# A hybrid decoder layer on one core: the mixers' TensorE order written out by hand

## The chip, the cores and the metric

The kernel runs on one core of a Trainium2 chip. The metric is the device time of one execution in microseconds. The kernel before took 2433.67 us (median of 3 runs, 2430.02 to 2435.79). One more execution was profiled. Engines are called PE (TensorE), DVE (VectorE), ACT (ScalarE), POOL (GpSimd) and SP (which issues the DMAs).

## What is computed

One decoder layer for 1024 prompt tokens and 8 x 8 sample tokens (1088 columns in all), model width 1024:

```
x = x + 1/2 * post1(SwiGLU_1(pre1(x)))
z = pre2(x) @ w_in                      # one input projection for everything below
branch A: sliding-window (128) attention, 8 heads on 2 key heads, with sinks
branch B: causal conv (width 4) and SiLU on q, k, v; gated DeltaNet, 4 heads of 128, chunks of 64
m = (sigmoid(gA) * (oA @ w_branch_a) + sigmoid(gB) * (oB @ w_branch_b)) @ w_out
x = x + post2(m)
x = x + 1/2 * post3(SwiGLU_2(pre3(x)))
```

Branch B solves, for each chunk and head, a unit lower triangular system, and then carries a 128 x 128 state S through the chunks:

```
sol = triangular_solve(I + M, [k * beta * exp(gc), v * beta])     # M strictly lower
v_new = v_u - k_cum @ S
o = q_dec @ S + (q k^T * decay) @ v_new
S = S * g_tot + k_dec^T @ v_new
```

## The kernel before, in words

All activations stand with features on partitions and the 1088 tokens along the free axis, in three chunks of 384, 384 and 320 columns (`CH`). Large products are made in three passes of split operands (high and low parts, lines 140 to 142 in `gemm`); the products of attention and of the delta heads are full-precision ones.

The kernel has five stages: the first FFN, keys, values and queries (lines 717 to 728), the mixers (834 to 1352), the branch and output projections (1358 to 1420), the second FFN. The change lies in the mixers.

The input projection's other columns are handled in *units* of 128 columns: a unit loads two weight tiles, splits each on ACT (line 113) and DVE (114) and makes 24 products for each of the three chunks. `conv_unit` (964) does one of 12 q, k or v columns with the convolution (line 980 for its taps, 1008 for the SiLU), `z_unit` (1015) one of 4 output gates, `gate_unit` (1042) one of 16 branch gates.

Attention over the prompt (`attention_prompt`, 907) has 16 items (8 blocks of 128 queries, two groups of four heads). `att_s` makes an item's scores, adds the mask on DVE (862) and runs the softmax (819): a maximum (822) on DVE, exponents on ACT (828), the division by the sum on ACT (832). `att_o` transposes the probabilities on PE (883), copies them (888) and multiplies with the values (893). The program issues the scores of an item, then the output of the item before. `attention_sample` (916) does the same for the sample tokens, four small items one after the other.

`delta_head` (1047) does one head: transposes and norms of k, the decay matrices D (1105, exponents 1113 and 1114), q k and k k products (1102, 1122), the matrix M (1126). The 32 x 32 diagonal blocks of M go to DRAM and come back one block to a partition, 34 of them (1161 to 1165); 31 steps of two DVE operations (1180, 1186) invert them all at once; the inverse and its transpose go out and come back into the zeroed tiles L and U (1187 to 1198). Two rounds of products make 128 x 128 inverses of them (1211 to 1230), with U scaled chunk by chunk on DVE (1202) and ACT (1203). Then comes the scan over eight chunks:

```
1253-1255  p[:, 0:128]    = U v, then + M S
1257       vns (DVE)      = p[:, 0:128] * kds
1259       vn  (ACT)      = p[:, 0:128]
1260       p[:, 128:256]  = k vns
1263       S2  (DVE)      = S * gtot + p[:, 128:256]
1270-1271  po[:, 0:128]   = S q, then + vn QK      # a PSUM tile of its own
1272       QK  (ACT)      = po[:, 0:128]
```

The sample tokens follow (1276 to 1309) and the gated norm (1311 to 1323), which ends with a product on POOL and a store (`obd`).

What sets the order: a scheduler of the framework places every instruction of every engine by its priority (program order, with some raised) and by a model of when its inputs are ready. So PE's order in the mixers is a mix that it chooses: gemm products of later units stand among the full-precision products of attention and of the heads. The program's order is attention, then head by head conv units, delta head, and z and gate units between (1329 to 1352). Only in attention do extra dependencies fix the order of some products. PSUM: three tiles for gemms (`pa`), two each of `ph` and `py`, one `po`; heads 0 and 2 use `ph` alone, heads 1 and 3 `py` alone.

Of the kernel before, what the change touches and what calls it, by code (L numbers as in the profile page):

```python
# [35 lines left out]
def body(ctx: ExitStack, tc: tile.TileContext, d):  # L36
# [23 lines left out]
    bd = [dp.tile([34, 32, 32], F32, tag=f"bd{i}", name=f"bd{i}") for i in range(12)]  # L60
# [758 lines left out]
    def softmax(s3, sk, sm):  # L819
        j = s3.shape[1]  # L820
        m, neg, e, l, r = (sm[:, 4 * i : 4 * i + j] for i in range(5))
        nc.vector.tensor_reduce(out=m, in_=s3, op=ALU.max, axis=AX.X)
        nc.vector.tensor_tensor(out=m, in0=m, in1=sk, op=ALU.max)
        nc.vector.tensor_tensor(out=e, in0=sk, in1=m, op=ALU.subtract)
        nc.vector.tensor_scalar_mul(neg, m, -1.0)
        nc.scalar.activation(e, e, AF.Exp)
        for i in range(j):
            nc.scalar.activation(s3[:, i, :], s3[:, i, :], AF.Exp, bias=neg[:, i : i + 1], accum_out=l[:, i : i + 1])
# [5 lines left out]
    items = [(n, tp2) for n in range(8) for tp2 in range(2)]  # L834
    pos = {}
    masked = []
    SYNC = mybir.DependencyInfo(mybir.DependencyClass.Sync, mybir.DependencyReason.DATA)
    NOSYNC = mybir.DependencyInfo(mybir.DependencyClass.NoSync, mybir.DependencyReason.DATA)
    chain = []
    half2 = (slice(0, 64), slice(64, 128))  # L840

    def att_s(it):
        n, tp2 = items[it]
        k0 = 128 if n == 0 else 0
        ps = (ph(), py())
        for j in range(2):
            for g2, hs in enumerate(half2):
                mm = nc.tensor.matmul(
                    ps[g2][:, j * 256 + k0 : j * 256 + 256],
                    YA[tp2 * 2 + j][hs, n * P : n * P + P],  # L850
                    kT[hs, (n - 1) * P + k0 : (n + 1) * P],
                    start=True,
                    stop=True,
                )
                if masked:
                    tc.add_manual_dep(mm.ins, masked[-1], SYNC, reason="both halves start together")
                if chain:
                    tc.add_manual_dep(mm.ins, chain[-1], NOSYNC, reason="halves in turn")
                chain.append(mm.ins.name)
        s4 = sbs[it % 2][:, :1024].rearrange("p (h k) -> p h k", k=256)[:, :, k0:256]  # L860
        for g2 in range(2):
            mask = nc.vector.tensor_tensor(
                out=s4[:, 2 * g2 : 2 * g2 + 2, :],
                in0=ps[g2].rearrange("p (j k) -> p j k", k=256)[:, :, k0:256],
                in1=cst[:, C_AM + k0 : C_AM + 256].unsqueeze(1).to_broadcast([P, 2, 256 - k0]),
                op=ALU.add,
            )
        masked.append(mask.ins.name)
        softmax(s4, vec[:, V_SK + 4 * tp2 : V_SK + 4 * tp2 + 4], st())

    def att_o(it):
        n, tp2 = items[it]
        sb = sbs[it % 2]
        if n not in pos:
            pos[n] = po_tile()
        po = pos[n]
        h2s = (1,) if n == 0 else (0, 1)
        pt = (ph(), py())
        for g2 in range(2):
            for h2 in h2s:  # L880
                for j in range(2):
                    c0 = (2 * g2 + j) * 256 + h2 * P
                    mm = nc.tensor.transpose(pt[g2][:, h2 * 256 + j * P : h2 * 256 + j * P + P], sb[:, c0 : c0 + P], ident)
                    tc.add_manual_dep(mm.ins, chain[-1], NOSYNC, reason="behind the scores")
                    chain.append(mm.ins.name)
        ptb = pts[it % 2]
        copies = [
            nc.scalar.copy(ptb[:, g2 * 512 + h2s[0] * 256 : g2 * 512 + 512], pt[g2][:, h2s[0] * 256 : 512]) for g2 in range(2)
        ]
        for h2 in h2s:  # L890
            blk = n - 1 + h2
            for g2, hs in enumerate(half2):
                mm = nc.tensor.matmul(
                    po[hs, tp2 * 256 : tp2 * 256 + 256],
                    vtok[:, blk * P + hs.start : blk * P + hs.stop],
                    ptb[:, g2 * 512 + h2 * 256 : g2 * 512 + h2 * 256 + 256],
                    start=h2 == h2s[0],
                    stop=h2 == 1,
                )
                tc.add_manual_dep(mm.ins, copies[1].ins.name, SYNC, reason="both halves start together")  # L900
                tc.add_manual_dep(mm.ins, chain[-1], NOSYNC, reason="halves in turn")
                chain.append(mm.ins.name)
        if tp2 == 1:
            for t in range(4):
                nc.scalar.copy(YA[t][:, n * P : n * P + P], po[:, t * P : t * P + P])

    def attention_prompt():
        for it in range(len(items)):
            att_s(it)
            if it > 0:  # L910
                att_o(it - 1)
        att_o(len(items) - 1)
        for t in range(4):
            nc.sync.dma_start(oad[t, :, :NPR], YA[t][:, :NPR])

    def attention_sample():
        kc, vc = YA[5], YA[7]
        nc.sync.dma_start(vc[:, :NPR].rearrange("p (b c) -> p b c", c=P), d["vc"].rearrange("b k c -> k b c"))
        nc.sync.dma_start(kc[:, :NPR].rearrange("p (b c) -> p b c", c=P), d["kc"])
        pos = po_tile()  # L920
        for it in range(4):
            bg2, g2 = it // 2, it % 2
            lo, hi = 64 * g2, 64 * g2 + 64
            ps = py()
            for b4 in range(4):
                b = bg2 * 4 + b4
                ql = qs[lo:hi, b, :, :].rearrange("p t k -> p (t k)")
                nc.tensor.matmul(ps[32 * b4 : 32 * b4 + 32, 0:128], ql, kc[lo:hi, b * P : b * P + P], start=True, stop=True)
                nc.tensor.matmul(ps[32 * b4 : 32 * b4 + 32, 128:192], ql, kT[lo:hi, NPR:NT], start=True, stop=True)
            sb = YA[6][:, it * 256 : it * 256 + 192]  # L930
            nc.vector.tensor_tensor(out=sb[:, 0:128], in0=ps[:, 0:128], in1=cst[:, C_SMC : C_SMC + P], op=ALU.add)
            nc.vector.tensor_tensor(
                out=sb[:, 128:192], in0=ps[:, 128:192], in1=cst[:, C_SMN + bg2 * NSM : C_SMN + bg2 * NSM + NSM], op=ALU.add
            )
            softmax(sb.unsqueeze(1), vec[:, V_SKS + g2 : V_SKS + g2 + 1], st())
            pt = py()
            nc.tensor.transpose(pt[:, 0:128], sb[:, 0:128], ident)
            nc.tensor.transpose(pt[:NSM, 128:256], sb[:, 128:192], ident)
            ptb = YA[0][:, it * 256 : it * 256 + 256]
            nc.scalar.copy(ptb[:, 0:128], pt[:, 0:128])  # L940
            nc.scalar.copy(ptb[:NSM, 128:256], pt[:NSM, 128:256])
            nc.tensor.matmul(
                pos[lo:hi, bg2 * 128 : bg2 * 128 + 128], vts[:, lo:hi], ptb[:NSM, 128:256], start=True, stop=False
            )
            for b4 in range(4):
                b = bg2 * 4 + b4
                nc.tensor.matmul(
                    pos[lo:hi, bg2 * 128 + 32 * b4 : bg2 * 128 + 32 * b4 + 32],
                    vc[:, b * P + lo : b * P + hi],
                    ptb[:, 32 * b4 : 32 * b4 + 32],  # L950
                    start=False,
                    stop=b4 == 3,
                )
        obs = YA[1][:, :256]
        nc.vector.tensor_copy(
            obs.rearrange("p (t b k) -> p t b k", t=4, b=8), pos[:, :256].rearrange("p (b t k) -> p t b k", t=4, b=8)
        )
        nc.sync.dma_start(oad[:, :, NPR:NT].rearrange("t p q -> p t q"), obs.rearrange("p (t q) -> p t q", t=4))


    ncv = s2b.tile([P, 12, 3], F32, tag="ncv", name="ncv")
    nc.vector.memset(ncv, 0.0)

    def conv_unit(u, dst):
        w = unit(U_QKV + u, f"qkv{u}")
        cw = [vec[:, V_CW + u * 4 + j : V_CW + u * 4 + j + 1] for j in range(4)]
        for c, (a, b) in enumerate(CH):
# [4 lines left out]
            gemm(ps, w, xn2, c)  # L972
# [39 lines left out]
    eps4 = s2b.tile([P, 1], F32, tag="eps4", name="eps4")  # L1012
    nc.vector.memset(eps4, 4.0 * P * EPS * EPS)

# [324 lines left out]
    for i in range(0, 2):  # L1339
        gate_unit(i)  # L1340
# [210 lines left out]
```

## Time and profile before

| | us |
|---|---|
| median of 3 runs | 2433.67 |
| the profiled execution | 2440.89 |
| its span, first to last instruction | 2439.1 |
| mixers, first score product to last gate product | 851 to 1474 |

In the lines below, `L1186` is line 1186 of the kernel before. A row of the groups gives line, engine, operation, output and inputs by name, shapes, count, then busy time and mean ns of one, then the idle time of the engine before them and what ended it. A row of the stretches gives the stretch and its length, then PE, PE's weight loads, DVE, ACT and POOL (busy us and instructions), then the granted share of the PE clock, the DMA share and GB/s. A row of the timeline gives start, length, engine, line and operation. A full-precision 128 x 128 product leaves two records, so the timeline shows it as x2.

### The profile page before, as it was taken

How to read it: one execution, taken by the hardware profiler on the slowest of the kernel's cores; microseconds unless marked ns; L12 is line 12 of the kernel's file. 1: busy time of each engine (PE TensorE's matmuls, PEld its weight loads, DVE VectorE, ACT ScalarE, POOL GpSimd, SP SyncE). 2: the span in 40 equal slices, each digit the busy share in tenths (PEclk: the TensorE clock that was granted, in tenths of full speed). 3: DMA queues.
4: the chain of work that ended last, by engine and by line, in shares of the span. 5: the costliest groups of instructions: out<-in, count | busy, mean ns of one | idle time of the engine just before them, and what ended most of it. 6: DMA issues, size and time to landing. Idle time of an engine off the chain costs nothing.

```text
span 2439.1 us, 38987 instructions
## 1 busy us (share of the span) xinstructions
PE 2373.7 (97%) x14535; PEld 2291.1 (94%) x14535; DVE 1704.9 (70%) x3519; ACT 1127.3 (46%) x2344; POOL 50.9 (2%) x36
## 2 busy tenths in 40 slices
PE   8999999999999999989999999999999999999997
PEld 7999999999998988888898899999999999999997
DVE  8887657757788576679697226556997576676677
ACT  7644423323465478634544333246654333233344
POOL 0000000000000000011111000000000000000000
PEclk9999999999999999999999999999999999999998
DMA  8332212213453311322223345435532122122453
GB/s 270 121 117 87 69 51 86 70 51 96 166 187 125 123 40 46 105 75 85 94 79 102 94 157 167 130 117 204 164 98 93 57 74 78 52 78 81 154 166 132
DMA packets 161558, 264.67 MB, mean 109 GB/s; under 512 B 35028, under 2 KB 66232, under 8 KB 161360
## 3 DMA queue, kind: packets, MB, share of 16 engines
q1 hardware_dynamic: 161368, 262.18, 33.3%
q8 instruction: 114, 1.87, 0.3%
q14 instruction: 76, 0.62, 0.1%
HBM read 223.88 MB, written 39.21 MB: 108 GB/s over the span
## 4 chain that ended last, share of the span: by engine, by line
PE 48%; DVE 6%; DMA 1%; ACT 1%; issue 1%; SPq 0%; POOL 0%; DVEq 0%; ACTq 0%; POOLq 0%
PE pa L140 7%; PE pa L142 7%; PE pa L141 7%; PE pa L464 4%; PE pa L465 4%; PE pa L466 4%; PE ph L346 2%; PE ph L347 2%; PE py L347 2%; PE py L346 2%; PE py L345 2%; PE ph L345 2%; DVE s L1186 1%; DVE s L1180 1%; DVE t L980 1%
## 5 line engine op out<-in xcount | busy, mean ns | idle before, releaser
L464 PE MATMUL pa<-ch,h_c_s 128*128 128x384 f32 x704 | 237.4, 337 | 4.3 <-DVE t L470 3.9
L465 PE MATMUL pa<-cl,h_c_s 128*128 128x384 f32 x704 | 236.4, 336 | 4.7 <-DVE cl L274 4.7
L466 PE MATMUL pa<-ch,l_c_s 128*128 128x384 f32 x704 | 236.3, 336 | 0.0
L470 DVE TENSOR_TENSOR t<-pa,t 128x384 f32<-128x384 f32 x308 | 170.0, 553 | 84.4 <-PE pa L466 84.3
L464 PE MATMUL pa<-ch,h_c_a 128*128 128x384 f32 x528 | 177.1, 335 | 1.2 <-ACT t L382 0.8
L466 PE MATMUL pa<-ch,l_c_a 128*128 128x384 f32 x528 | 176.7, 335 | 0.0
L465 PE MATMUL pa<-cl,h_c_a 128*128 128x384 f32 x528 | 176.6, 335 | 0.0
L113 ACT CAST h_c_a<-r_c_a 128x512 fp32r<-128x512 f32 x132 | 81.8, 620 | 131.5 <-PE pa L465 113.3
L464 PEld LDWEIGHTS pa<-ch,h_c_s 128*128 128x128 f32 x704 | 132.9, 189 | 7.9 <-DVE t L470 7.4
L465 PEld LDWEIGHTS pa<-cl,h_c_s 128*128 128x128 f32 x704 | 133.0, 189 | 4.9 <-DVE cl L274 4.9
L466 PEld LDWEIGHTS pa<-ch,l_c_s 128*128 128x128 f32 x704 | 132.9, 189 | 0.0
L113 ACT CAST h_c_s<-q_c_s 128x512 fp32r<-128x512 f32 x132 | 82.0, 621 | 106.4 <-PE pa L465 95.8
L140 PE MATMUL pa<-xbh,h_ga 128*128 128x384 f32 (+1 forms) x384 | 129.3, 337 | 0.0
L142 PE MATMUL pa<-xbh,l_ga 128*128 128x384 f32 (+1 forms) x384 | 128.8, 335 | 0.0
L141 PE MATMUL pa<-xbl,h_ga 128*128 128x384 f32 (+1 forms) x384 | 128.3, 334 | 0.0
L464 PEld LDWEIGHTS pa<-ch,h_c_a 128*128 128x128 f32 x528 | 99.1, 188 | 2.1 <-ACT t L382 1.1
L466 PEld LDWEIGHTS pa<-ch,l_c_a 128*128 128x128 f32 x528 | 99.1, 188 | 0.0
L465 PEld LDWEIGHTS pa<-cl,h_c_a 128*128 128x128 f32 x528 | 99.1, 188 | 0.0
L140 PE MATMUL pa<-xbh,h_qkv 128*128 128x384 f32 (+1 forms) x288 | 96.7, 336 | 0.0
L141 PE MATMUL pa<-xbl,h_qkv 128*128 128x384 f32 (+1 forms) x288 | 96.4, 335 | 0.0
L142 PE MATMUL pa<-xbh,l_qkv 128*128 128x384 f32 (+1 forms) x288 | 96.2, 334 | 0.0
L113 ACT CAST h_c_s<-r_c_s 128x512 fp32r<-128x512 f32 x44 | 27.4, 623 | 147.7 <-PE pa L465 135.7
(615 smaller groups left out, 7340.9 us busy)
## 6 DMA issues: line engine op xcount, KB each, us to landing
r_c_a<-in_up_dram SPq DMA_DIRECT2D x132, 256.0 KB
q_c_a<-in_up_dram SPq DMA_DIRECT2D x44, 256.0 KB
q_ub<-in_up_dram SPq DMA_DIRECT2D x44, 256.0 KB
r_ub<-in_up_dram SPq DMA_DIRECT2D x44, 256.0 KB
r_ua<-in_up_dram SPq DMA_DIRECT2D x42, 256.0 KB
q_ua<-in_up_dram SPq DMA_DIRECT2D x42, 256.0 KB
r_da<-in_dn_dram SPq DMA_DIRECT2D x40, 256.0 KB
q_da<-in_dn_dram SPq DMA_DIRECT2D x40, 256.0 KB
```

The lines of the kernel that those rows point to most:

```text
L113: nc.scalar.copy(hi, full)
L140: nc.tensor.matmul(ps[:, :n], hi[:, j, :], at(xh, k), start=first, stop=False)
L141: nc.tensor.matmul(ps[:, :n], hi[:, j, :], at(xl, k), start=False, stop=False)
L142: mm = nc.tensor.matmul(ps[:, :n], lo[:, j, :], at(xh, k), start=False, stop=last)
L345: nc.tensor.matmul(ps[:, :n], hi[:, i, :], hh, start=i == 0, stop=False)
L346: nc.tensor.matmul(ps[:, :n], hi[:, i, :], hl, start=False, stop=False)
L347: nc.tensor.matmul(ps[:, :n], lo[:, i, :], hh, start=False, stop=i == len(hs) - 1)
L464: nc.tensor.matmul(ps, wh[:, k, :], xh[:, k, :], start=k == 0, stop=False)
L465: nc.tensor.matmul(ps, wh[:, k, :], xl[:, k, :], start=False, stop=False)
L466: nc.tensor.matmul(ps, wl[:, k, :], xh[:, k, :], start=False, stop=k == 3)
L470: nc.vector.tensor_tensor(out=out, in0=ps, in1=other, op=ALU.add)
L980: nc.vector.scalar_tensor_tensor(out=acc[:, :m], in0=pre[:, j : j + m], scalar=cw[j], in1=acc[:, :m], op0=ALU.mult, op1=ALU.add)
```

## The change

PE's order in the mixers is written by hand: the block runs under `manual_schedule` for PE, so that PE's instructions keep the program's order. The other engines and the DMAs are still ordered by the scheduler.

- Units become generators that yield after each k step of a chunk (three products) the time it is counted at. A queue of units is worked off by `fill(us)`, which takes steps from the first unit of the queue until that much time is counted, and by `finish`, which runs units to their end.
- Attention runs as a pipeline of three items: scores of item `it`, values of `it-2`, transposes of `it-1`, then a fill of 4.8. The division by the sum moves from ACT to one DVE product with a broadcast. The sample part makes all four scores and softmaxes, then all transposes, then all value products, with fills of 3.0, 8.0 and 2.0.
- The delta heads run in pairs (0 and 1, 2 and 3). Each head is two generators, `first` (to the matrix M and the transposed v) and `second` (the rest), and `together` advances both heads of a pair step by step. The number that a step yields is the fill behind it: 2.0 once in `first`, 2.0, 2.0 and 5.0 in `second`, 0.0 elsewhere, through the whole scan.
- One inversion serves a pair: 68 blocks on 68 partitions, with a fill of 46.0. The inverse goes to DRAM tiles that hold whole 128 x 128 matrices (zeroed once at the start, eight stores of 0.5 MB) and L and U are read back as whole rows. The inverse's tiles no longer overlap L and U; each head has a second half-tile (R2).
- In `second`, both halves of a head (four chunks each) go through each step before the next one. One DVE product with a broadcast replaces four scalings of line 1202. In the scan, the next chunk's U v product stands ahead of the k product, and the outputs go to columns 256 to 384 of the same PSUM tile.
- PSUM tiles of the heads alternate between `ph` and `py`.

Its core (unchanged or merely moved lines left out):

```diff
+    def gemm_p(ps, w, c):
+        for k in range(KT):
+            gemm(ps, w, xn2, c, ks=(k,), ends=(k == 0, k == KT - 1))
+            yield 0.0013 * width(c) + 0.04
+    def fill(us):
+        while us > 0 and queue:
+            t = next(queue[0], None)
+            if t is None:
+                queue.pop(0)
+            else:
+                us -= t
...
-        for i in range(j):
-            nc.scalar.mul(s3[:, i, :], s3[:, i, :], r[:, i : i + 1])
+        nc.vector.tensor_tensor(out=s3, in0=s3, in1=r.unsqueeze(2).to_broadcast(list(s3.shape)), op=ALU.mult)
...
+        for it in range(n + 2):
+            if it < n:
+                att_s(it)
+            if it >= 2:
+                att_v(it - 2)
+            if 1 <= it <= n:
+                att_t(it - 1)
+            fill(4.8 if it else 7.0)
...
+            def uv(c):
+                w, cs, ix = chunk_of(c, h)
+                ps[c] = pb()
+                nc.tensor.matmul(ps[c][:, 0:128], U[:, cs], v[:, cs], start=True, stop=c == 0)
+            uv(0)
+            yield 0.0
+            for c in range(8):
+                w, cs, ix = chunk_of(c, h)
+                p = ps[c]
+                if c > 0:
+                    nc.tensor.matmul(p[:, 0:128], M[:, cs], S, start=False, stop=True)
+                vns = ar[:, c % 2, :]
+                nc.vector.tensor_scalar_mul(vns, p[:, 0:128], tk["kds"][:, ix : ix + 1])
+                vn = ar[:, 2 + c % 2, :]
+                nc.scalar.copy(vn, p[:, 0:128])
+                yield 0.0
+                if c < 7:
+                    uv(c + 1)
+                yield 0.0
+                nc.tensor.matmul(p[:, 128:256], k[:, cs], vns, start=True, stop=True)
+                S2 = ar[:, 4 + c % 2, :]
...
+                if c > 0:
+                    nc.tensor.matmul(p[:, 256:384], S, q[:, cs], start=True, stop=False)
+                nc.tensor.matmul(p[:, 256:384], vn, QK[:, cs], start=c == 0, stop=True)
+                nc.scalar.copy(QK[:, cs], p[:, 256:384])
+                S = S2
+                yield 0.0
...
+    def together(a, b):
+        for us in zip(a, b):
+            fill(max(us))
...
+        for i, x in enumerate(heads):
+            h, L, U = x.h, x.A[1], x.A[5]
+            nc.sync.dma_start(blocks32(ud[h]), Md[34 * i : 34 * i + 32])
+            nc.sync.dma_start(bu[h][32:34], Md[34 * i + 32 : 34 * i + 34])
+            nc.sync.dma_start(blocks32(ld[h]), Ld[34 * i : 34 * i + 32])
+            nc.sync.dma_start(U[:, :NPR].rearrange("p (c s) -> p c s", s=P), whole_rows(ud[h]))
+            nc.sync.dma_start(L[:, :NPR].rearrange("p (c s) -> p c s", s=P), whole_rows(ld[h]))
...
+        fill(46.0)
...
+    with tc.manual_schedule(engines={mybir.EngineType.PE}):
+        queue += zs[0:2] + gates[0:3] + heads[0].conv
+        attention_prompt()
+        attention_sample()
+        queue += heads[1].conv
+        for hs in (heads[0:2], heads[2:4]):
+            finish(list(queue))
+            queue += gates[3:9] if hs[0].h == 0 else gates[9:]
+            together(*(x.first() for x in hs))
+            invert(hs)
+            together(*(x.second() for x in hs))
+            if hs[0].h == 0:
+                finish(list(queue))
+                queue += zs[2:4] + heads[2].conv + heads[3].conv
+        finish(list(queue))
+        wg4 = [unit(U_GA + i, f"ga{i}") for i in range(14, 16)]
+        for c in range(3):
+            for i in range(2):
+                drain(gate_do(14 + i, wg4[i], c))
```

More of the change, by code (lines that the diff above doesn't have):

```diff
@@ L59, in body @@
     zd = dp.tile([4, P, NT], F32, tag="zd", name="zd")
[L60 removed]
+    bm, bu = ([dp.tile([34, 32, 32], F32, tag=f"{n}{h}", name=f"{n}{h}") for h in range(4)] for n in ("bm", "bu"))
+    ld, ud = ([dp.tile([8, 4 * 4128], F32, tag=f"{n}{h}", name=f"{n}{h}") for h in range(4)] for n in ("ld", "ud"))
     yd = [dp.tile([P, 4, width(2)], F32, tag=f"yd{i}", name=f"yd{i}") for i in range(2)]
@@ L830, in softmax @@
         nc.vector.reciprocal(r, l)
-        for i in range(j):
-            nc.scalar.mul(s3[:, i, :], s3[:, i, :], r[:, i : i + 1])
[L834 to L958, printed above, removed]
@@ L964, in conv_unit, with finish @@
+    def finish(units):
+        for u in units:
+            if u in queue:
+                queue.remove(u)
+                drain(u)
     def conv_unit(u, dst):
@@ L971, in conv_unit @@
             ps = pa()
-            gemm(ps, w, xn2, c)
+            yield from gemm_p(ps, w, c)
             pre = t1()
@@ L1019, in z_unit @@
             ps = pa()
-            gemm(ps, w, xn2, c)
+            yield from gemm_p(ps, w, c)
             z = t1()
@@ L1031, in gate_do @@
         ps = pa()
-        gemm(ps, w, xn2, c)
+        yield from gemm_p(ps, w, c)
         z = t1()
@@ new lines, in gate_unit, with att_s @@
+            yield from gate_do(i, w, c)
+    items = [(n, tp2) for n in range(8) for tp2 in range(2)]
+    pos = {}
+    masked = []
+    probs = {}
+    half2 = (slice(0, 64), slice(64, 128))
+    def att_s(it):
+        n, tp2 = items[it]
+        k0 = 128 if n == 0 else 0
+        ps = (ph(), py())
+        for j in range(2):
+            for g2, hs in enumerate(half2):
+                mm = nc.tensor.matmul(
+                    ps[g2][:, j * 256 + k0 : j * 256 + 256],
+                    YA[tp2 * 2 + j][hs, n * P : n * P + P],
+                    kT[hs, (n - 1) * P + k0 : (n + 1) * P],
+                    start=True,
+                    stop=True,
+                )
+                if masked:
+                    tc.add_manual_dep(mm.ins, masked[-1], SYNC, reason="both halves start together")
+        s4 = sbs[it % 2][:, :1024].rearrange("p (h k) -> p h k", k=256)[:, :, k0:256]
+        for g2 in range(2):
+            mask = nc.vector.tensor_tensor(
+                out=s4[:, 2 * g2 : 2 * g2 + 2, :],
+                in0=ps[g2].rearrange("p (j k) -> p j k", k=256)[:, :, k0:256],
+                in1=cst[:, C_AM + k0 : C_AM + 256].unsqueeze(1).to_broadcast([P, 2, 256 - k0]),
+                op=ALU.add,
+            )
+        masked.append(mask.ins.name)
+        softmax(s4, vec[:, V_SK + 4 * tp2 : V_SK + 4 * tp2 + 4], st())
@@ new lines, in att_t @@
+    def att_t(it):
+        n, tp2 = items[it]
+        sb = sbs[it % 2]
+        h2s = (1,) if n == 0 else (0, 1)
+        pt = (ph(), py())
+        for g2 in range(2):
+            for h2 in h2s:
+                for j in range(2):
+                    c0 = (2 * g2 + j) * 256 + h2 * P
+                    nc.tensor.transpose(pt[g2][:, h2 * 256 + j * P : h2 * 256 + j * P + P], sb[:, c0 : c0 + P], ident)
+        ptb = pts[it % 2]
+        probs[it] = [
+            nc.scalar.copy(ptb[:, g2 * 512 + h2s[0] * 256 : g2 * 512 + 512], pt[g2][:, h2s[0] * 256 : 512]) for g2 in range(2)
+        ]
@@ new lines, in att_v @@
+    def att_v(it):
+        n, tp2 = items[it]
+        if n not in pos:
+            pos[n] = po_tile()
+        po = pos[n]
+        h2s = (1,) if n == 0 else (0, 1)
+        ptb = pts[it % 2]
+        for h2 in h2s:
+            blk = n - 1 + h2
+            for g2, hs in enumerate(half2):
+                mm = nc.tensor.matmul(
+                    po[hs, tp2 * 256 : tp2 * 256 + 256],
+                    vtok[:, blk * P + hs.start : blk * P + hs.stop],
+                    ptb[:, g2 * 512 + h2 * 256 : g2 * 512 + h2 * 256 + 256],
+                    start=h2 == h2s[0],
+                    stop=h2 == 1,
+                )
+                tc.add_manual_dep(mm.ins, probs[it][1].ins.name, SYNC, reason="both halves start together")
+        if tp2 == 1:
+            for t in range(4):
+                nc.scalar.copy(YA[t][:, n * P : n * P + P], po[:, t * P : t * P + P])
@@ new lines, in body, with wide, blocks32, whole_rows @@
+    ncv = s2b.tile([P, 12, 3], F32, tag="ncv", name="ncv")
+    nc.vector.memset(ncv, 0.0)
+    eps4 = s2b.tile([P, 1], F32, tag="eps4", name="eps4")
+    nc.vector.memset(eps4, 4.0 * P * EPS * EPS)
+    def wide(t, c0):
+        return t[:, c0 * P : c0 * P + 512]
+    def blocks32(t):
+        return t.rearrange("c (b q) -> (c b) q", q=4128)[:, : 32 * P].rearrange("g (r s) -> g r s", s=P)[:, :, 0:32]
+    def whole_rows(t):
+        return t[:, : P * P].rearrange("c (r s) -> r c s", s=P)
+    nc.gpsimd.memset(HA[5], 0.0)
@@ new lines, in first @@
+            nc.gpsimd.tensor_tensor(out=M3, in0=M3, in1=cst[:, C_OFF : C_OFF + P].unsqueeze(1).to_broadcast([P, 8, P]), op=ALU.mult)
+            nc.gpsimd.memset(U[:NSM, NPR:], 0.0)
+            yield 0.0
+            for c0 in (0, 4, 8):
+                n = 4 if c0 < 8 else 1
+                w = P if c0 < 8 else NSM
+                p = pb()
+                for i in range(n):
+                    nc.tensor.transpose(p[:w, i * P : i * P + P], v[:, (c0 + i) * P : (c0 + i) * P + w], ident)
+                nc.scalar.copy(wide(v, c0) if c0 < 8 else v8, p[:w, : n * P])
@@ new lines, in invert @@
+        fill(46.0)
+    heads = [Head(h, (HA, YA)[h % 2]) for h in range(4)]
+    zs = [z_unit(h) for h in range(4)]
+    gates = [gate_unit(i) for i in range(14)]
+    with tc.manual_schedule(engines={mybir.EngineType.PE}):
[17 more added lines that the diff above has]
+                drain(gate_do(14 + i, wg4[i], c))
```

580 lines of the change are left out of this document (304 added, 276 removed).

## The prediction

> **What bounds the kernel now.** First the page's engine totals, then the same by stretches.
>
> ```profile
> span 2439.1 us, 38987 instructions
> PE 2373.7 (97%) x14535; PEld 2291.1 (94%) x14535; DVE 1704.9 (70%) x3519; ACT 1127.3 (46%) x2344; POOL 50.9 (2%) x36
> ```
> ```profile
> 851.00:1476.00 625.00, 601.17 (x3878) 540.95 (x3878) 416.30 (x1189) 329.49 (x822) 50.74 (x32) 0.98 0.29 91
> 851.00:980.00 129.00, 125.91 (x824) 105.44 (x824) 88.69 (x265) 103.03 (x320) 0.00 (x0) 1.00 0.13 42
> 1360.00:1476.00 116.00, 116.00 (x722) 108.89 (x721) 40.29 (x79) 46.56 (x103) 4.45 (x2) 1.00 0.44 141
> ```
>
> TensorE carries the whole span, and in the last stretch, which ends with gates alone, it has no idle time. The mixers, which alone change, run from the first score at 851 to the last gate product at 1474: 623 us. "Busy" is no peak, since products overlap. The pace is read in the timeline, from start to start.
>
> ```profile
> 1442.69 0.33 PE L141 MATMUL pa<-xbl,h_ga 128*128 128x384 f32 x1
> ...
> 1447.03 0.33 PE L142 MATMUL pa<-xbh,l_ga 128*128 128x384 f32 x1
> ```
> ```profile
> 1112.26 0.39 PE L1255 MATMUL ph<-s,s 128*128 128x128 f32 x2
> 1112.48 0.39 PE L1270 MATMUL ph<-s,s 128*128 128x128 f32 x2
> ```
>
> 25 steps of 384 columns in 4.34 us are 0.174 each, 320 columns at that rate 0.145; a full-precision 128x128 product (two records) is 0.22. A unit (one weight column: 24 products for each of two chunks of 384 and one of 320) is 48 x 0.174 + 24 x 0.145 = 11.8 us, and 32 units (12 conv, 4 z, 16 gate) are 379. A delta head has 86 products of 0.22, 18.9 us, and at the same rate per column about 9.7 of transposes, narrow and 512-wide products: 114 for four heads. Attention at that rate is 40, its sample part and the value transposes 10. Together 543 us (an estimate at the pace of these rows). So 80 of the 623 us are lost today. The waits of TensorE name only part of it:
>
> ```profile
> PE py L1119 <- ACT s L1114: 7.1, 2, 4.7
> PE py L1215 <- ACT s L1212: 3.2, 1, 3.2
> PE py L1211 <- DMA s<-bd: 2.6, 1, 2.6
> ```
>
> All named waits come to some 23 us; the rest is spread thin, about 0.1 us wherever a product's operand has only just come or gemm and full-precision products change places. The change can win at most the 80, and loses what its fixed TensorE order cannot cover. I count its waits part by part against 543, so none can be below nothing.
>
> **Attention.** Item it's scores, item it-2's values, item it-1's transposes, then gemm steps worth 4.8; a 384 step is priced at 0.539 and takes 3 x 0.174 = 0.52, so 4.7 us. Scores, values and transposes are 2.6 us of an item (40 over 15 to 16), and four changes of kind at about 0.09 make 7.6 us an iteration: 6 us of changes over 18.
>
> ```profile
> L980 DVE SCALAR_TENSOR_TENSOR t<-t,vec,t 128x384 f32<-128x384 f32 (+1 forms) x108 | 60.1, 562 | 2.2 <-ACT t L978 2.2
> L1180 DVE TENSOR_TENSOR s<-s,s 34x31 f32<-34x31 f32 (+15 forms) x124 | 43.4, 350 | 3.0 <-DMA s<-bd 1.4
> L1186 DVE TENSOR_TENSOR s<-s,s 34x31 f32<-34x31 f32 (+15 forms) x124 | 42.9, 346 | 1.6
> ```
> ```profile
> L1008 DVE SCALAR_TENSOR_TENSOR s<-t,t 128x384 f32<-128x384 f32 (+1 forms) x36 | 18.9, 527 | 6.6 <-ACT t L1007 6.1 <-PE po L947 0.4
> L1105 DVE SCALAR_TENSOR_TENSOR s<-s,tk_gc,cst 128x128 f32<-128x128 f32 x32 | 13.1, 426 | 1.3 <-DMA s<-gcd 1.3
> ```
> ```profile
> L822 DVE TENSOR_REDUCE st<-s 128x4 f32<-128x1024 f32 x14 | 17.0, 1213 | 0.1
> L862 DVE TENSOR_TENSOR s<-ph,cst 128x512 f32<-128x512 f32 x14 | 9.6, 684 | 2.9 <-PE py L848 2.8
> L1314 DVE TENSOR_TENSOR s<-s,s 128x1088 f32<-128x1088 f32 x4 | 5.1, 1279 | 0.0
> L828 ACT ACTIVATE s<-s,st 128x256 f32<-128x256 f32 x56 | 27.7, 496 | 0.0
> L828 ACT ACTIVATION_READ_ACCUMULATOR s<-s,st 128x1 f32 x68 | 12.7, 187 | 0.0
> ```
>
> The division leaves ACT for DVE: one 1024-wide product, 1.2 by L1314 (1088 wide). The softmax chain is then 2 x 0.68 + 1.21 + about 0.5 small + 4 x (0.50 + 0.19) + 0.3 + 1.2 = 7.3, with hand-overs about 7.8; between an item's scores and its transposes TensorE has 0.95 + 0.9 + 4.7 + 0.95 + 0.95 = 8.5 us of other work. That just holds with z and gate fills: I take 3 us for twelve items. The last five to six fills are conv units, whose DVE share is by the rows (60.1 + 18.9)/12 = 6.6 from two lines alone and with the small operations 10 to 12, so 4.5 a fill; with the softmax's 4.5 DVE has 9.0 us in a 7.6 us iteration: 8 us lost. 11 in all (bounds 0 and 25).
>
> **Sample part.** The fills so far have used some 95 of the queue's 98 us, so the fill of 8.0 behind four softmaxes finds about 3, and DVE still has conv work: 9 us lost (0 to 13).
>
> **Conv of head 1, first halves.** Three conv units need 31 to 36 us of DVE for 36 of TensorE: 2. Then both heads' first half: DVE has per head 8 x 0.43 (L1105), eight more 128-wide operations with an operand in PSUM, four 512-wide ones of about 0.68 (like L862) and small ones; I estimate 12, so 24 a pair, against 14 us of TensorE and a fill of 2.0. I take 9 for the first pair, and 5 for the second, whose decay exponents can run during the long gemm run ahead of it (2 to 15 each).
>
> **Substitution.** The 62 steps are chained, (43.4 + 42.9)/4 = 21.6 us a head, 22.9 with gaps; a pair now shares one run, so DVE saves 46 us in all. But TensorE doesn't end on DVE today: only 1.4 us of waits before L1180 and 2.6 before L1211 come from this loop, so the saving itself I cost at nothing. The DMA steps around it:
>
> ```profile
> 1290.02 0.93 SPq L1161 DMA_DIRECT2D bd<-s  x2
> ...
> 1295.05 0.24 SPq L1165 DMA_DIRECT2D s<-bd  x1
> ```
> ```profile
> 1341.63 0.24 SPq L1190 DMA_DIRECT2D bd<-s  x1
> ...
> 1344.63 0.81 SPq L1195 DMA_DIRECT2D s<-bd  x2
> ```
>
> From the last write of a matrix's blocks to the first step I take 5.5 us, by the 5.0 of the first pair of rows; a read can follow a write after 3 (second pair). The chain of a pair: 5.5; 23 plus about 7 of gate splits; the transposing copy 1.9; write, landing and the first read 8. That is 45 us against a fill of 44.4 that starts some 3 us earlier: 4 lost (0 to 12). On SP the reads wait for the landing with gate weights behind them, which run some units ahead. The inverse now comes back as whole rows, four tensors of 512 KB, at
>
> ```profile
> 1367.90:1370.40 2.50, 2.50 (x19) 2.17 (x19) 0.44 (x2) 2.39 (x9) 0.00 (x0) 1.00 0.74 215
> ```
>
> 215 GB/s: 2.5 us each, so head b's first products wait 3.3 more. The eight zero writes (0.5 MB each, 20 us of DMA at this rate) go through SP ahead of the mixers' weights; nothing shows their place: 0 to 20, taken as 0, since DMA is 13% used in 851 to 980.
>
> **Second halves.** Up to the scan, 3.3 for head b as said, and
>
> ```profile
> L1203 ACT ACTIVATE s<-s,nk 128x128 f32<-128x128 f32 x32 | 10.4, 392 | 2.5 <-DVE s L1202 2.5
> ```
>
> sixteen of these scalings (6.3 us of ACT) stand ahead of the copies that free PSUM for head b's last products, under a fill of 2.0; about 8 a pair in all. Then the scan. Today gemm products fill one head's chain:
>
> ```profile
> 1112.69 0.35 DVE L1257 TENSOR_SCALAR s<-ph,tk_kds 128x128 f32<-128x128 f32 x1
> ```
> ```profile
> 1110.55 0.27 ACT L1259 COPY s<-ph 128x128 f32<-128x128 f32 x1 [0.54 <-DVE s L1257]
> 1110.88 0.47 PE L1260 MATMUL ph<-s,s 128*128 128x128 f32 x2
> 1111.40 0.35 DVE L1263 SCALAR_TENSOR_TENSOR s<-s,tk_gtot,ph 128x128 f32<-128x128 f32 x1
> ```
> ```profile
>   ACT s L1259: 5.2, 21
> ```
>
> The last row says what L1260 waited for: the copy of L1259, whose result it does not read. They only share a PSUM tile (other columns), and ACT's copy itself starts when DVE's read of that tile is over. So accesses of one tile go one after another. The change puts the output products (state by q, new values by QK) into this same tile, behind the state update that reads it on DVE; today they have a tile of their own (po). Per step of a pair: a's product with the state 0.39, scaling 0.35, copy 0.27, with gaps to 1.15; k product 0.47, to 1.62; state update to 2.01; only then a's two output products, 2.07 to 2.61; then b's k product, update and output products in the same way, 2.61 to 3.97. TensorE has 10 x 0.22 = 2.2 us of work in these 4.0, and no fill stands inside (all are 0.0). Eight steps are 31 us for 17 of work: 14 lost a pair. If the output products were not held, a step would be 2.55 and the loss 3. The tail costs 1.5 a pair.
>
> **The rest.** Six conv units in one gemm run: 3. The end: 27 us of gates cover the last norms and the reload of 1.5 MB, 2. Sum of waits: 11 + 9 + 2 + 9 + 5 + 2 x (4 + 8 + 14 + 1.5) + 3 + 2 = 96. The stage becomes 543 + 6 + 96 = 645 us, 22 more than 623. The profiled execution took 2440.89 us, 7.2 over the median of the runs (2433.67); it would be 2463, and the median 2456.
>
> **Rivals.** *Faster:* the fixed order covers its waits. For it speak the 57 us of thin losses today, 46 us less of DVE, and that bounds of several terms are near 0. If the output products aren't held (21 less) and half of the 34 us in attention, sample and first halves is covered, 2456 - 38 = 2418, with 2402 where nearly all is. Against it: the scan's tile rule is in 21 waits. *No change:* only the output products aren't held: 2456 - 21 = 2435. *Slower still, by the clock:*
>
> ```profile
> 994.64:998.05 3.41, 2.05 (x25) 1.44 (x24) 3.29 (x20) 3.28 (x6) 0.08 (x1) 1.00 0.64 246
> 998.05:1004.88 6.83, 6.83 (x45) 5.46 (x43) 1.56 (x7) 3.26 (x11) 0.00 (x0) 0.50 0.27 77
> 1021.89:1025.30 3.41, 2.07 (x12) 2.03 (x12) 3.27 (x12) 2.42 (x6) 0.00 (x0) 1.00 0.77 232
> 1025.30:1028.70 3.40, 3.40 (x22) 3.36 (x22) 3.36 (x9) 2.78 (x5) 0.00 (x0) 1.00 0.35 130
> ```
>
> A window 60% busy was followed by 6.8 us at half clock, another of 61% was not: the point of decision lies near there. The scan is about 75% busy by its records but 55% by its work. At half clock a step is about 5.5 us, so 2 x 7.5 x 1.5 = 22 more: 2478. The Trainium skill ("TensorE: Matmul & The Clock Gate", section "A second HAM failure mode: psum-queue depth-cycling") says that many micro-idles between groups of products, from cycling PSUM, can make the clock swing between half and full; by that rule this rival would happen. The two pairs of rows leave it open. The change fixes TensorE's order alone; that ACT, DVE or SP order themselves worse than assumed lies in the range.
>
> **How the numbers follow.** The forecast, 2456 (2440 to 2472 by itself), has 0.46; the clock rival 0.12; no change 0.10; faster 0.32. A measurement of this kernel can tell about 0.2%, 5 us. Slower is 0.46 + 0.12 = 0.58. The range reaches from the faster rival's end, 2402, to 2490, the clock rival plus some of the zero writes; what lies outside I give 0.2.
>
> **What would show it.** Right: scan steps of a pair of about 4 us with output products waiting for the state update on DVE; substitution 62 steps, twice; waits of TensorE on DVE in the first halves; a stage of about 645 us. Wrong: scan steps of 2.5 us, a fill of 46 that ends after the inverse has landed, or gemm steps dense through attention.

## The result, and the profile after

| | before | after |
|---|---|---|
| median of the runs, us | 2434.46 (2430.02 to 2435.79, 4 runs) | 2465.63 (2460.59 to 2467.94, 4 runs) |
| ratio to before, 95% interval | | 1.0128, 1.0108 to 1.0149 |
| profiled execution, its span, us | 2440.89, 2439.1 | 2460.59, 2458.8 |
| mixers, first score to last unit product, us | 851.0 to 1474.1: 623 | 849.9 to 1489.9: 640 |

The change makes the kernel slower by 31 us in the medians. The two profiles show 20 of them, because the profiled execution of before took 6 us more than the median of its runs, and that of after 5 us less than its own.

First the head of the page of after, then the engines' busy time by stretches of the mixers. The columns are the stretch and its length, the busy time (and instructions) of PE, PEld, DVE, ACT and POOL, the granted clock, the DMA share and GB/s.

```profile
span 2458.8 us, 38753 instructions
PE 2372.7 (96%) x14535; PEld 2302.1 (94%) x14535; DVE 1691.8 (69%) x3385; ACT 1098.7 (45%) x2272; POOL 42.9 (2%) x33
```
```profile
849.90:1489.80 639.90, 597.57 (x3867) 549.80 (x3867) 394.22 (x1039) 291.47 (x730) 41.68 (x28) 0.97 0.28 86
849.90:1001.70 151.80, 147.59 (x1003) 128.44 (x1002) 103.89 (x252) 86.20 (x274) 1.32 (x1) 0.97 0.22 70
1001.70:1020.00 18.30, 11.62 (x68) 8.35 (x66) 12.60 (x63) 8.15 (x30) 0.33 (x2) 0.69 0.28 97
1056.80:1077.30 20.50, 17.45 (x140) 15.62 (x138) 19.87 (x67) 12.93 (x32) 6.12 (x5) 1.00 0.14 35
1151.10:1181.60 30.50, 22.27 (x145) 17.89 (x146) 9.71 (x30) 7.83 (x30) 0.00 (x0) 1.00 0.12 39
1181.60:1206.20 24.60, 24.59 (x106) 19.38 (x105) 8.51 (x14) 6.95 (x13) 3.79 (x2) 0.79 0.35 108
1206.20:1316.10 109.90, 109.90 (x672) 109.90 (x671) 81.72 (x216) 57.21 (x103) 6.69 (x6) 1.00 0.28 92
1411.10:1441.60 30.50, 22.28 (x145) 17.90 (x146) 9.71 (x30) 7.84 (x30) 0.00 (x0) 1.00 0.12 39
1441.60:1463.20 21.60, 21.59 (x107) 16.63 (x105) 8.51 (x14) 6.99 (x13) 3.79 (x2) 0.92 0.40 122
```

The stretches are, in this order: all of the mixers, attention, sample part, the first pair's first halves, its scan, its tail, the long gemm run, and the second pair's scan and tail. The two scans take 30.5 us each. TensorE is idle in 8 us of each by its records, and no other engine is busy for more than 10 us: a chain runs from engine to engine. In the first halves DVE is the bound (19.87 of 20.50). The long run has no gap. The pauses in the sample part are followed by half clock (0.69), and the first tail, which starts when the scan is over, is at 0.79. By the clock records of the two traces, the mixers lie at half clock for 44 us in all, against 27 before. What that adds is at most half of the difference, some 8 of the 17 us by which the stage is longer (an estimate).

The waits of TensorE that are new or have grown, from the view of its waits (total, times, longest):

```profile
PE ph L1237 <- DMA s<-ud: 7.3, 4, 2.9
PE ph L1323 <- DVE s L1317: 6.2, 14, 0.4
PE py L1323 <- DVE s L1317: 6.2, 14, 0.4
...
PE ph L1046 <- DVE s L833: 3.9, 1, 3.9
...
PE ph L979 <- DVE s L833: 3.1, 2, 2.9
```

L1323 is the output product of state by q, and L1317 the state update, whose result it does not read. It waits in all 28 steps that have an update. L1046 and L979 are the transposes of attention, which before had waited 2.1 and 2.5 us for the division on ACT. One step of a pair from the timeline (start, duration, tile, releaser):

```profile
1158.54 0.49 PE L1314 MATMUL ph<-s,s 128*128 128x128 f32 x2
1159.47 0.49 PE L1323 MATMUL ph<-s,s 128*128 128x128 f32 x2 [0.44 <-DVE s L1317]
1159.79 0.39 PE L1324 MATMUL ph<-s,s 128*128 128x128 f32 x2
1160.01 0.39 PE L1314 MATMUL py<-s,s 128*128 128x128 f32 x2
1160.84 0.49 PE L1323 MATMUL py<-s,s 128*128 128x128 f32 x2 [0.44 <-DVE s L1317]
...
1162.57 0.49 PE L1314 MATMUL ph<-s,s 128*128 128x128 f32 x2
```

From one k product of head a (`ph`) to the next are 4.03 us. Twice in a step TensorE stands before an output product. From a k product's start to the output's it takes 0.93 and 0.83 us; without the wait (own_tile, below) it is 0.32 and 0.22.

### The profile page after: what moved, and what is told of

It is laid out like the page before. It is cut to its first block, busy times and chain, and to the rows that moved or that the text cites. A ratio compares the mean times of both kernels' runs of the same rounds, so it can differ in the third digit from the quotient of the medians.

```text
span 2458.8 us, 38753 instructions
## 1 busy us (share of the span) xinstructions
PE 2372.7 (96%) x14535; PEld 2302.1 (94%) x14535; DVE 1691.8 (69%) x3385; ACT 1098.7 (45%) x2272; POOL 42.9 (2%) x33
```

## The experiments

All ratios are to the kernel before. "After" stands for 1.0128. A stage length is counted from the first score to the last product of a unit, in the timeline of the run.

**own_tile.** In the scan of after:

```
+ po = pa()
- matmul(p[:, 256:384], S, q ...); matmul(p[:, 256:384], vn, QK ...); copy(QK, p[:, 256:384])
+ matmul(po[:, 0:128], S, q ...);  matmul(po[:, 0:128], vn, QK ...);  copy(QK, po[:, 0:128])
```

> The changed kernel with one edit: the scan's output products (state by q, new values by QK) go into a PSUM tile of their own (one of the three gemm tiles, free in the scan). Theory (accesses of one PSUM tile go one after another, so the outputs wait for the state update on DVE): a step of the pair falls from 4.0 to about 2.6 us, 16 steps give about 21 us back, 2445 us or 1.004 of the kernel before. Rival (the step is bound by the order or by DVE and ACT themselves, and the wait only moves to the next product): steps stay near 4.0, 2461 to 2468.

Measured 1.0009 (0.9995 to 1.0023), 2438.23 us; the span falls by 21.0 to 2437.8. The same step in its timeline:

```profile
1157.35 0.49 PE L1314 MATMUL ph<-s,s 128*128 128x128 f32 x2
1157.67 0.39 PE L1324 MATMUL pa<-s,s 128*128 128x128 f32 x2
1157.89 0.39 PE L1325 MATMUL pa<-s,s 128*128 128x128 f32 x2
1158.12 0.39 PE L1314 MATMUL py<-s,s 128*128 128x128 f32 x2
...
1159.97 0.49 PE L1314 MATMUL ph<-s,s 128*128 128x128 f32 x2
```

The outputs now follow the k product at TensorE's own pace, and a step is 2.62 us. The stretch and the tail behind it:

```profile
1152.60:1171.90 19.30, 18.32 (x144) 16.99 (x145) 9.71 (x30) 7.86 (x30) 0.00 (x0) 1.00 0.18 57
1171.90:1193.70 21.80, 21.68 (x107) 16.69 (x105) 8.85 (x15) 6.96 (x13) 3.79 (x2) 0.92 0.40 126
```

The scan is 11.2 us shorter than in after, and the tail 2.8, since it lies less at half clock. Two scans and this tail make 25 us, more than the 21.0 of the spans. Meanwhile half clock grew in the sample part and in the second pair (48 us of it in the mixers here, 44 in after). The shared tile was the largest of the losses that the prediction lists. The Trainium skill ("Perfetto Trace Analysis", section "Matmuls") advises that independent groups of products rotate through different PSUM banks, so that the reading of one overlaps the products of the next. The two traces agree, with 4.03 us shared and 2.62 apart.

**update_last.** In after, the state update (DVE) is moved behind the two output products; the tile stays shared.

> The changed kernel with the state update on DVE moved behind the two output products in program order; the tile is shared as before. Theory (one access after another, in program order): the outputs are released by the product with k alone, the update comes about 0.5 us later; a step of the pair is about 2.9 us, some 18 us back, 2448 us. Rival (what counts is that one tile holds both, in either order): the update is now what waits, the step stays at 3.8 to 4.0, 2461 to 2468.

Measured 1.0021 (1.0007 to 1.0035), 2442.87 us. The step is 2.78 us:

```profile
1159.16 0.39 PE L1314 MATMUL ph<-s,s 128*128 128x128 f32 x2
1159.38 0.39 PE L1317 MATMUL ph<-s,s 128*128 128x128 f32 x2
1159.60 0.39 PE L1318 MATMUL ph<-s,s 128*128 128x128 f32 x2
1159.83 0.39 PE L1314 MATMUL py<-s,s 128*128 128x128 f32 x2
...
1161.17 0.49 PE L1305 MATMUL py<-s,s 128*128 128x128 f32 x2 [0.18 <-DVE s L1320]
...
1161.94 0.39 PE L1314 MATMUL ph<-s,s 128*128 128x128 f32 x2
```

(Here L1317 and L1318 are the output products and L1320 is the update.) So it is the order of the accesses to the tile that counts. With the three products of TensorE first, what is left of the wait is 0.18 us at head b's next product with the state, which does read the update's result. The Trainium skill ("PSUM — Partial Sum Buffer", section "PSUM bank collisions raise a hardware error") says that the compiler back end adds a dependency between any two instructions of different engines that touch the same bank and quadrant, reads included. The waits of after agree, and their disappearance here shows the cost to be one of order.

**before_shared.** The opposite edit in the kernel before: its outputs go to columns 256 to 384 of the shared tile.

> The kernel before with one edit: the scan's output products go into the same PSUM tile as the rest of the step (columns 256 to 384), as the change does. Theory (the gemm products that stand in the scan there cover a held product): within 5 us of the kernel before, 2430 to 2440. Rival (the shared tile costs 1.4 us a step of a head wherever it stands, 32 steps): about 2470 or more.

Measured 0.9985 (0.9973 to 0.9997), 2433.3 us. Only one held output shows in the waits:

```profile
PE py L1269 <- DVE s L1263: 0.6, 1, 0.6
```

With gemm products between the scan's products the same tile costs nothing. The cost belongs to tile and written order together.

**free_order.** After, with the line that fixes TensorE's order taken out.

```
- with tc.manual_schedule(engines={mybir.EngineType.PE}):
+ if True:
```

> The changed kernel with TensorE's order left to the scheduler instead of the written one; pairs, buffers, softmax division and shared tile stay. Theory (what the change loses, it loses because nothing is moved into the waits of a fixed order): gemm products go into the scan and the other gaps, 2425 to 2445. Rival (the loss comes with the pairs and the buffers, whatever the order): 2455 to 2475 or more.

Measured 0.9929 (0.9902 to 0.9957), 2424.01 us. By the ratio that is 17 us under the kernel before, and better than the theory's 2425 to 2445, which is 9 under to 11 over. A step of its scan:

```profile
1147.78 0.39 PE L1305 MATMUL ph<-s,s 128*128 128x128 f32 x2
...
1148.59 0.42 PE L143 MATMUL pa<-xbl,h_ga 128*128 128x384 f32 x1
1148.96 0.49 PE L1314 MATMUL ph<-s,s 128*128 128x128 f32 x2
1149.20 0.42 PE L144 MATMUL pa<-xbh,l_ga 128*128 128x384 f32 x1
1149.46 0.38 PE L1314 MATMUL py<-s,s 128*128 128x128 f32 x2
1149.60 0.42 PE L142 MATMUL pa<-xbh,h_ga 128*128 128x384 f32 x1
1149.88 0.49 PE L1323 MATMUL ph<-s,s 128*128 128x128 f32 x2
...
1150.88 0.39 PE L1305 MATMUL ph<-s,s 128*128 128x128 f32 x2
```

The scheduler puts both k products ahead of both outputs, and a gemm product into each of three gaps. A step is 3.10 us, 0.52 of them gemm work, and the wait on L1317 is gone from the view of waits. So the rest of the change (pairs, buffers, the single substitution, attention in another program order) is a gain when taken together; its parts were not tried one by one. The written order, with this tile, costs 0.0199 x 2434 = 48 us.

**free_own.** free_order, with the outputs in the one tile that attention uses for its values.

> The run free_order (ratio 0.993) with the scan's outputs in the tile that attention uses for its output (one, for both heads of a pair). Theory (where gemm products stand between the scan's products, a held output costs nothing): within 4 us of free_order, ratio 0.991 to 0.995. Rival (a quarter of the 21 us that own_tile won remains to be won here): 0.990 or less.

Measured 0.9907 (0.9891 to 0.9924), 2412.04 us, the fastest of all. Its interval overlaps that of free_order, so the tile is worth little there; whether it is worth 5 us isn't settled.

**fill51.** own_tile, `fill(46.0)` in `invert` made `fill(51.0)`, pairs fed by `gates[3:8]` and `gates[8:]`.

> The changed kernel with the scan's outputs in a tile of their own (the run own_tile, ratio 1.0009) and the fill behind the substitution raised from 46 to 51; one gate unit moves from the first pair to the second so that the queue lasts. Theory (the fill ends before the inverse is back; the four waits on the reload, 8.1 us in own_tile, are covered by work that would otherwise come later): about 8 us less, ratio 0.998. Rival (more fill pulls more weights through SP ahead of the reload, or the wait only moves to the second head's transfers): within 3 us of own_tile, ratio 1.000 to 1.002.

Measured 0.9960 (0.9945 to 0.9975), 2425.56 us: 12 us less than own_tile by the ratios. The wait on the reload of the inverse (L1237, 8.1 us in own_tile) is gone from the view of waits. The 4 us beyond the theory lie within the intervals of the two ratios.

**queue_sample.** own_tile, first queue `gates[0:4]` for `gates[0:3]`, first pair `gates[4:9]`.

> own_tile with one more gate unit in the queue that feeds the attention, so that the fill of 8.0 in the sample part is served in full. Theory (the sample part loses because its queue has run dry, and the pause brings half clock after it): most of the 12 us lost there go, 8 to 10 us less, ratio 0.997. Rival (the sample part is bound by DVE, which still has the convolution of the units before): the product still waits for the softmax division, 0 to 3 us less, ratio 1.000.

Measured 0.9956 (0.9941 to 0.9971), 2425.27 us: 13 less. Of the wait of the sample part on its softmax this is left:

```profile
PE ph L1046 <- DVE s L833: 0.8, 1, 0.8
```

where own_tile has 4.2 us. DVE was late, but by less than the fill covers: the missing piece was TensorE work in the queue. Two more things came with it. The extra unit stands ahead of the conv units, so that these come later, and the wait of attention at L979 falls from 3.1 to 0.2 us. The half clock around the sample part falls from 17 us to 7. So the 13 us are not the sample part's alone.

**combo.** own_tile with both, and more fills: in each scan step 0.5, in the tail 1.5 for 0 and 3 for 2, in the first halves 5 for 2, before the last inverse products 4 for 2; `zs[2:4]` go from the long run to the first pair.

> own_tile with the longer queue for the sample part, the fill of 51, one gemm step (0.52 us) inside each scan step of a pair, longer fills in the first halves (5 for 2), ahead of the last inverse products (4 for 2) and in the tail (1.5 for 0, 3 for 2); the last two z units move into the first pair's queue. Theory (every wait of the fixed order can be covered by gemm steps that otherwise run later): 8 for the inverse, 9 for the sample part, 8 for the scan, 5 for tail and first halves, about 28 us less than own_tile, 2410 us, ratio 0.990. Rival (the chains are bound by DVE and ACT, to which the fills add splits and evictions, so that fills only lengthen them): 10 us less at most, ratio 0.997 or above.

Measured 0.9951 (0.9931 to 0.9970), 2424.75 us. No gain is left over fill51 or queue_sample alone; the theory fails here. The scan did become dense:

```profile
1160.00:1172.00 12.00, 12.00 (x101) 12.00 (x100) 5.36 (x17) 4.65 (x18) 0.00 (x0) 1.00 0.07 23
1270.00:1300.00 30.00, 23.21 (x146) 22.49 (x146) 23.94 (x74) 18.56 (x38) 5.58 (x6) 0.91 0.20 68
1455.00:1475.00 20.00, 13.98 (x69) 12.73 (x67) 16.16 (x34) 11.69 (x26) 0.00 (x0) 0.92 0.85 272
```

But 7 us are lost in the second pair's first halves (second row) and 6 where the branch stage starts (third row). The waits there:

```profile
PE ph L1129 <- ACT s L1131: 4.9, 2, 3.9
PE ph L1175 <- DVE s L1178: 3.8, 2, 1.9
```

They were 1.9 us (L1129) in own_tile, and L1175 wasn't named there. But own_tile too sits idle in these places, 3.1 us in the second pair's first halves and 3.7 at the start of the branch stage, so only some 6 us of the 13 are new. That the work used for the new fills was missing there, or the z units' place in particular, wasn't tried by itself.

**best_fixed.** own_tile with the edits of fill51 and queue_sample alone (`gates[0:4]`, then five units a pair).

> The written TensorE order with three edits together: outputs in a tile of their own, the fill of 51, and the longer queue for the sample part (the first queue takes gates 0 to 3, each pair five more); none of the other fills of combo, and the last z units stay in the long gemm run. Theory (the three gains lie in different stretches and add up; what combo lost, it lost by its fills and by taking the z units out of the long run, under which the second pair's exponents were computed): 1.0009 - 0.0049 - 0.0053 = 0.991, some 2414 us. Rival (the gains of fill51 and queue_sample overlap, as combo's 0.995 says): 0.994 to 0.996.

Measured 0.9915 (0.9891 to 0.9939), 2414.87 us: the two gains add up. A written order beats the kernel before, too, and is level with free_own.

**best_free.** free_own with the same two edits.

> free_own (ratio 0.991) with the fill of 51 and the longer first queue. Theory (with the order left to the scheduler, the written fills set only priorities, and the scheduler has filled the same gaps by itself): within 4 us of free_own, 0.989 to 0.993. Rival (more gemm work ahead of the sample part and behind the substitution helps in any order): 0.987 or less.

Measured 0.9923 (0.9902 to 0.9943), 2417.37 us: level with free_own. The scheduler needs no help with these gaps.

**zero_three.** After, with the eight zero writes issued three times.

> The changed kernel with the eight zero writes of 0.5 MB issued three times, 8 MB more ahead of the mixers' weights. Theory (DMA has room there, and the weights run units ahead): within 3 us of the changed kernel, ratio 1.011 to 1.014. Rival (4 MB more take the weights' turn on SP, up to 20 us of DMA each time): 10 to 40 us more, ratio 1.017 or above.

Measured 1.0189 (1.0153 to 1.0226), 2479.01 us, some 15 us slower than after. The theory fails:

```profile
PE pa L142 <- ACT h_z L115: 11.0, 1, 11.0
```

The first fill waits for the split of its weights, which came late. After has no such wait: its eight writes are issued from 807 to 823 us and fit in, but the room ahead of the mixers' weights isn't as large as I thought.

**division_act.** After, with the softmax division as four ACT scalings (`nc.scalar.mul`) again.

> The changed kernel with the softmax division back on ScalarE (four scalings of 256 columns instead of one DVE product of 1024). Theory (the attention waits where conv units load DVE; 1.2 us of DVE less an item, 0.8 us more of chain): the two waits on the division, 7 us, shrink, 0 to 4 us less, ratio 1.011 to 1.013. Rival (the chain's length decides, which stood at 7.8 of 8.5 us): 8.6 us against 8.5 in every item, up to 10 us more, ratio 1.015 or above.

Measured 1.0114 (1.0088 to 1.0141), 2464.84 us: no difference from after that can be told. The attention's wait on the division falls from 3.1 us (L979 in after) to 1.0 (L980 here):

```profile
PE ph L1047 <- ACT s L834: 4.3, 2, 4.0
...
PE ph L980 <- ACT s L834: 1.0, 2, 0.7
```

The sample part's wait (L1047 here, L1046 in after) stays, now on ACT. The place of the division makes no difference that these runs can tell.

## Why the prediction was right

The forecast was slower: a stage of 645 us, an execution of 2463 for the profiled one, a median of 2456. The profiled stage is 640 and its execution 2460.59. Part by part, with the losses counted as in the prediction (start to start, against TensorE's pace):

- **Scan: 4.0 us per step, 14 us lost a pair.** The mechanism and the size were right: 4.03 us and 13 lost. own_tile and update_last show the cause in two ways. The 2.55 us forecast without the hold was 2.62. The 21 us for both pairs was 22.4 in the two scans and 21.0 in the spans, where other stretches changed too. By the ratios it was 0.0119 x 2434 = 29; 6 of the 8 us between come from the profiled runs, of which after's lay 5 below its median and own_tile's 1 above.
- **Attention, 6 + 11.** About 17 us lost, as predicted in sum, but this is luck, since they were not lost as said. The iterations with conv fills were forecast at 9.0 us, with DVE as the bound; the three that can be read from one item's scores to the next took 7.8 to 8.3, hardly more than the ones before them once the pipeline is full (7.4 to 8.2, forecast 7.6). The one long wait on the division, 2.9 us at 977 us, does come in the conv fills, as said. And 10 us of the stretch lie at half clock (851.8 to 858.6 and 978.1 to 981.5), which the sum had not priced.
- **Sample part, 9.** Direction right, size too small: 12, since the pause also brought half clock (0.69 in 18.3 us), which the sum had not priced. The queue had run dry, and with one more unit in it the wait is nearly gone (queue_sample).
- **Conv of head 1, 2; first halves, 9 and 5.** 1.4 for the conv units. The first halves lost 5 and 5.5: DVE needed 20 us a pair where I had estimated 24.
- **Inverse and early second halves, 4 + 8 a pair.** Direction right, size too large: about 8 lost in each pair, where 12 were forecast. The inverse was late, and waits on its reload show it, but they come to 7.3 us in the two pairs together. The forecast had 4 a pair for the inverse and 3.3 for head b's transfers, 14.6 in all.
- **Tail, 1.5 a pair.** Mis-sized: about 7.5 and 4.1, with half clock in it (0.79 and 0.92).
- **The conv run, 3, and the end, 2.** 0.3 and nothing; but the branch stage then waits 3.8 us for DVE (L1467), which wasn't forecast (the span grew 3 us more than the stage).
- **The zero writes, 0.** No wait shows for one set; the reason given, that DMA has room, was too generous (zero_three).
- **The sum.** These losses come to some 95 us for the 102 forecast, and 543 + 95 = 638 for a measured stage of 640. Sample part and tails lost 12 us more than forecast, inverse, first halves, scans and the last terms some 19 less. So 645 came near 640 in part because misses cancelled.
- **From the profile to the median.** This step failed: I took off 7.2 us because before's profiled run lay that far over its median. After's lay 5 below its own. These 12 us, less the 2.4 by which the profiled execution came out below its forecast, are the 10 between the forecast and the measured median.

**The rivals.** "No change", by outputs that are not held, is what own_tile made: 1.0009. The faster rival's 2418 is what the same change gives once the tile is no longer shared, the fill behind the substitution is longer and the queue of the sample part has one more unit (best_fixed, 2414.87), or with the order left free. How much of that is the thin losses of before and how much the shorter work of DVE, no run tells apart. The clock rival did not come in the scan, where it was placed: the granted clock is 1.00 in both scans of after, although the PSUM tiles cycle with pauses of 0.4 us. The rule of the Trainium skill on PSUM-queue cycling ("TensorE: Matmul & The Clock Gate", section "A second HAM failure mode: psum-queue depth-cycling") is not borne out at this density of work (22.27 us busy in 30.50). Half clock came elsewhere: at the start and end of attention, in and behind the sample part, in the second halves ahead of the scans, and in the tails, where it set in 1.3 us behind the first scan and 4.1 behind the second. Whether the scans' pauses brought it there no run tells; own_tile's denser scans are followed by it too. Nor does the point of decision near 60% busy, which the prediction read from two windows, hold: the 3.4 us ahead of the half clock in the two tails are 82% and 100% busy by the records.

## What to carry to other kernels

An order written by hand can turn a wait that it did not foresee into lost time, so read each PSUM tile's accesses in program order before writing it, and put products that need nothing from the other engine ahead of its read, or in another tile. Fills are work taken from elsewhere: lengthen those that a named wait asks for, and then look at the stretch from which the work was taken. When a sum comes out right, check its terms one by one, since misses can cancel. Before an edit is judged by one profile, compare how far each profiled run lies from its own median.

## What the runs showed that I had not expected

The same sharing of a PSUM tile cost 0.0119 of the time in a fixed order, and nothing with gemm products between (0.9985). 8 MB more of zero writes issued ahead of the stage held its first weights back by 11 us. The granted clock stayed at 1.00 through scans in which TensorE was busy for 73% of the time by its records, and fell in the sample part, which was 63% busy (11.62 of 18.30). But it fell too in the first tail, which was busy throughout (24.59 of 24.60), so the busy share of the records does not tell when it falls.
